# Attention's values as matmuls over two-part operands, and a paced output product

## The chip, the cores and the metric

The program runs on one NeuronCore of a Trainium2 chip. The metric is the time of one execution on the device in microseconds (us); lower is better. TensorE is called PE here, its weight loads PEld, VectorE DVE, ScalarE ACT, GpSimd POOL, and the DMA queue of SyncE SP.

## The reference, cut to what matters

The model is a two-layer trunk. In each layer one projection of the normalised input feeds three branches (a gated linear recurrence, sparse attention and a state-space scan), and one output product adds their concatenation to x:

```python
qg = qq.reshape(Bn, qb, N_KV_HEADS, G, ATT_HEAD_DIM)
logits = jnp.einsum('bqgrd,bqkgd->bqgrk', qg, ksel).astype(jnp.float32) * (ATT_HEAD_DIM ** -0.5)
...
p = jax.nn.softmax(logits, axis=-1)
o = jnp.einsum('bqgrk,bqkgd->bqgrd', p.astype(vsel.dtype), vsel)
...
y_b = o * jax.nn.silu(ga)
...
mix = jnp.concatenate([y_a, y_b, y_c], axis=-1)
x = x + jnp.einsum('bte,ed->btd', mix, p['w_out'].astype(mix.dtype)).astype(x.dtype)
```

There are 1024 prompt tokens and 64 sample tokens with 512 cached ones. Attention has 8 query heads in 2 key groups of 4, each 64 wide. The output product maps 2048 inputs to 1024 outputs for 1088 tokens.

## The kernel before

All values are float32. The large products run in PE's single-pass form (fp32r): an operand is split into a high part, rounded by a copy into an fp32r tile, and a low part, the rest, by a subtraction. `three` (lines 212 to 217) adds high by high, high by low and low by high into one PSUM bank. Attention's product of weights with values is not of this kind: it runs on float32 operands as they are.

Tokens come in chunks of 384, 384 and 320 columns (`CH`) for the projections, and in nine query tiles for attention: eight of 128 prompt tokens and one, tile 8, of 64 sample tokens.

A layer ends with attention and the output product. The output product is done in two halves (half 0 and half 1, or product 0 and product 1), each of 8 inputs of 128 rows: half 0 takes the recurrence's outputs and half of the scan's, which are ready before attention; half 1 takes the rest of the scan's and attention's. `y_tile` loads one input chunk and splits it into the tiles `Y` (names sth and stl in the profile: high and low; a holds chunks 0 and 1, b chunk 2). There is one set of these tiles, used by half 0 and then by half 1. `out_proj(half, ...)` goes over 8 blocks d of 128 outputs: `weights` loads and splits 128x1024 weights (whi by ACT, wlo by POOL), and for each chunk 24 matmuls go into a bank mm, which `add_x` (half 0) or `add_last` (half 1) adds to x.

Attention works on units of one query tile and one key group, 18 of them, in the order of `todo`: group 0 with tiles 1, 0, 2, 3, 4, 5, 8, 7, 6, then group 1 with 2, 1, 0, 3, 8, 4, 5, 6, 7. Tile t below 8 reaches 128 (t+1) keys, tile 8 reaches 576. `queries` transposes a unit's queries. `weigh` computes, for each of 4 heads, scores in PSUM (L1068), adds bias and mask and takes the minimum on DVE (L1071), exponentiates on ACT (L1075, with the sum), and scales by the reciprocal on DVE (L1077, L1078). `values` takes the weights 128 keys at a time: four transposes into a bank tp (L1093), a copy to pT on ACT (L1095), and the products with the values vt (L1098) into a bank s1; at the end DVE multiplies by the gate (L1100) and two DMAs store to ybd. Each L1098 product has 64 output rows and lies in one half of the array's columns: b = 0 and b = 1 write partitions 0 to 63 and 64 to 127.

The order of instructions on each engine is fixed before the run by a planner that simulates the program. The program's text gives priority: half 0 stands after all of attention, so its matmuls fill places where, in the planner's simulation, none of attention's is ready. Weights are given a higher priority (`high_priority`). The pool `p` has two buffers of each tile unless said otherwise; eight of lg, the 128x1024 tiles of weights. PSUM has three banks mm, two tp, two s2 (scores) and one s1.

## Time and profile before

| what | value |
|---|---|
| median of three runs | 2049.99 us (2048.08 to 2056.05) |
| the profiled execution | 2043.88 us, span 2042.1 us, mean granted clock 0.983 |
| busy share of the span | PE 96%, PEld 86%, DVE 74%, ACT 60%, POOL 32% |
| attention with half 0, layer 0 | about 690 to 948 us of the span |
| the same, layer 1 | about 1700 to 1955 us |

Times inside the span are counted from its first instruction. The busy time of PE is modelled: matmuls are pipelined and overlap, so that a busy PE can still have empty places; its weight loads show these better. A group's idle time is that of its engine just before it, with what ended it. An fp32 operand shows as f32, an fp32r one also as f32 on PE. An instruction of PE on an fp32 product appears twice.

### The profile page before, as it was taken

The page shows a single profiled execution, that of the slowest core. Times are in us where ns is not written, and L with a number is a line of the kernel's source. Part 1 is how long each engine was busy: PE and PEld are TensorE (multiplying, and loading weights), DVE is VectorE, ACT ScalarE, POOL GpSimd, SP SyncE. Part 2 cuts the span into 40 slices and gives each one's busy share as a digit, 9 for nine tenths or more (in the row PEclk, how much of TensorE's full clock was granted, in tenths as well). Part 3 has the DMA queues.
Part 4 walks back from the last instruction along what each step waited for, and adds up shares of the span by engine and source line. Part 5 has one row for each costly group of instructions (what it writes and reads, how often), then busy time and mean ns, then how long its engine had stood idle before and what let it go on. Part 6 is the DMA issues. An engine that isn't in the chain of part 4 may idle for free.

```text
span 2042.1 us, 34620 instructions
## 1 busy us (share of the span) xinstructions
PE 1952.6 (96%) x12056; PEld 1747.9 (86%) x12056; DVE 1519.2 (74%) x3701; ACT 1231.8 (60%) x2567; POOL 651.2 (32%) x561
## 2 busy tenths in 40 slices
PE   6999999989999899999999999999899999999999
PEld 5899989888889787866998999999888887888589
DVE  7778899898866855574386888999987678566723
ACT  6569988753656544454355798987446655444621
POOL 3012244333522422253430213353245224223320
PEclk9999999999999899999999999999999998999999
DMA  6125354535332732324541343545353346234145
GB/s 228 62 72 143 101 167 123 173 105 154 107 109 83 231 116 89 106 89 137 191 134 38 108 124 108 161 137 165 99 163 97 96 149 197 90 99 140 46 145 169
DMA packets 252079, 257.94 MB, mean 126 GB/s; under 512 B 31264, under 2 KB 230304, under 8 KB 251904
## 3 DMA queue, kind: packets, MB, share of 16 engines
q1 hardware_dynamic: 251904, 255.73, 40.9%
q8 instruction: 95, 1.56, 0.3%
q14 instruction: 80, 0.66, 0.1%
HBM read 181.09 MB, written 74.57 MB: 125 GB/s over the span
## 4 chain that ended last, share of the span: by engine, by line
PE 66%; DVE 19%; DMA 6%; ACT 5%; issue 3%; SPq 1%; POOL 0%; DVEq 0%; ACTq 0%
PE mm L216 16%; PE mm L215 15%; PE mm L217 15%; PE s L1098 4%; PE tp L1093 4%; PE s L1068 3%; DVE u L855 2%; ACT junka L580 2%; PE s L881 1%; DMA cumB<-cumd 1%; PE s L514 1%; DMA eB<-cumd 1%; ACT cumB L742 1%; DMA xsc<-xsd 1%; PE s L791 1%
## 5 line engine op out<-in xcount | busy, mean ns | idle before, releaser
L193 POOL TENSOR_TENSOR wlo<-wraw,whi 128x1024 fp32r<-128x1024 f32 x80 | 195.4, 2442 | 364.0 <-ACT whi L192 360.3
L580 ACT ACTIVATE junka<-sc,cand 128x768 bf16<-128x768 f32 x248 | 239.4, 968 | 8.5 <-DVE sc L583 3.9
L192 ACT ACTIVATE whi<-wraw 128x1024 fp32r<-128x1024 f32 x130 | 137.1, 1054 | 135.3 <-PE mm L216 109.8
L1075 ACT ACTIVATE lg<-lg,mx 128x512 f32<-128x512 f32 (+8 forms) x144 | 111.2, 773 | 95.7 <-DVE mx L1071 95.3
L855 DVE SCALAR_TENSOR_TENSOR u<-raw,parh,u 128x384 f32<-128x384 f32 (+1 forms) x198 | 147.4, 751 | 11.7 <-POOL u L853 5.9
L1095 ACT ACTIVATE pT<-tp 128x512 f32<-128x512 f32 (+1 forms) x164 | 90.5, 568 | 108.1 <-PE tp L1093 103.5
L1060 POOL TENSOR_TENSOR nbm<-nb,shared 128x256 f32<-128x256 f32 (+1 forms) x112 | 81.2, 730 | 224.1 <-DVE mx L1071 201.8
L574 DVE TENSOR_SCALAR_CACHE_REDUCE junk<-sc,cand 128x384 bf16<-128x384 f32 (+4 forms) x194 | 139.9, 753 | 1.0
L1068 PE MATMUL s<-kst,qst 128*128 128x512 f32 (+4 forms) x448 | 120.8, 362 | 7.8 <-DVE mx L1071 7.3
L742 ACT ACTIVATE cumB<-cumB,ctk 128x128 f32<-128x128 f32 (+1 forms) x288 | 88.4, 384 | 54.3 <-DMA cumB<-cumd 47.7
L1093 PEld LDWEIGHTS tp<-identr,lg 128*128 128x128 f32 (+2 forms) x656 | 71.8, 140 | 45.6 <-issue 39.4
L1093 PE MATMUL tp<-identr,lg 128*128 128x128 f32 (+2 forms) x656 | 107.2, 278 | 0.5 <-DVE lg L1078 0.5
L1098 PE MATMUL s<-pT,vt 128*64 128x256 f32 (+2 forms) x656 | 104.8, 389 | 1.6 <-ACT pT L1095 1.6
L1078 DVE TENSOR_SCALAR lg<-lg,ri 128x512 f32<-128x512 f32 (+8 forms) x144 | 93.6, 651 | 3.3
L1143 DVE TENSOR_TENSOR xl<-xl,mm 128x384 f32<-128x384 f32 (+1 forms) x40 | 21.4, 540 | 94.1 <-PE mm L217 84.9
L1068 PEld LDWEIGHTS s<-kst,qst 128*128 128x128 f32 (+1 forms) x448 | 72.2, 188 | 21.9 <-DVE mx L1071 13.4
L215 PE MATMUL mm<-sth0a,whi 128*128 128x384 f32 (+1 forms) x228 | 82.9, 365 | 7.3 <-DVE xl L1143 2.0
L1071 DVE CUSTOM_DVE_ANT_0 lg<-s,shared 128x512 f32<-128x512 f32 (+4 forms) x112 | 61.8, 553 | 37.7 <-PE s L1068 31.9
L193 DVE TENSOR_TENSOR wlo<-wraw,whi 128x1024 fp32r<-128x1024 f32 x50 | 64.1, 1281 | 32.1 <-ACT whi L192 32.0
L216 PE MATMUL mm<-stl1a,whi 128*128 128x384 f32 (+1 forms) x228 | 79.6, 349 | 3.8 <-DVE stl1a L954 3.5
L216 PE MATMUL mm<-stl0a,whi 128*128 128x384 f32 (+1 forms) x228 | 79.8, 350 | 2.4 <-POOL stl0a L954 2.0
L778 POOL TENSOR_TENSOR hT<-hT,dec 128x512 f32<-128x512 f32 x28 | 35.9, 1282 | 144.3 <-DVE hT L780 137.0
(475 smaller groups left out, 6931.1 us busy)
## 6 DMA issues: line engine op xcount, KB each, us to landing
wraw<-in_w_in_dram SPq DMA_DIRECT2D x82, 512.0 KB, 3.5
wraw<-in_w_out_dram SPq DMA_DIRECT2D x48, 512.0 KB, 3.8
cumB<-cumd SPq DMA_DIRECT2D x32, 512.0 KB, 4.8
xsd<-u SPq DMA_DIRECT2D x48, 192.0 KB, 2.4
gz<-gzd SPq DMA_DIRECT2D x32, 256.0 KB, 3.6
xsc<-xsd SPq DMA_DIRECT2D x32, 256.0 KB, 3.5
eB<-cumd SPq DMA_DIRECT2D x56, 128.0 KB, 4.1
gzd<-g SPq DMA_DIRECT2D x32, 192.0 KB, 1.9
```

Of the source, the lines that this page charges most:

```text
L192: S.activation(hi, raw, AF.Copy)
L193: eng.tensor_tensor(lo, raw, hi.bitcast(F32), op=OP.subtract)
L215: PE.matmul(ps, hi[:, k, :], xh[ci][:, c0:], start=k == 0, stop=False)
L216: PE.matmul(ps, hi[:, k, :], xl[ci][:, c0:], start=False, stop=False)
L217: PE.matmul(ps, lo[:, k, :], xh[ci][:, c0:], start=False, stop=k == len(xs) - 1)
L574: V.tensor_scalar(junk, sc[j][:n], thr, None, op0=op, op1=OP.add, accum_out=out)
L580: S.activation(junk, sc[j][:n], AF.Sign, scale=-1.0, bias=cand, accum_out=out)
L855: V.scalar_tensor_tensor(u, raw[:, j:j + n], w[:, wbase + j * wstride:wbase + j * wstride + 1], u, op0=OP.mult, op1=OP.add)
L1068: PE.matmul(ps[:nq, :b - a], qst[:, h, :nq], kst[:, g, pt, kbase + a:kbase + b], start=pt == 0, stop=pt == 1)
L1075: S.activation(lg[:nq, :nk], lg[:nq, :nk], AF.Exp, scale=-1.0, bias=mx[:nq, h, k_ - 1:k_], accum_out=sm[:nq, h:h + 1])
L1093: PE.transpose(ps[:n, i * nq:(i + 1) * nq], lgs[h][:nq, j * 128:j * 128 + n], ident[:nq, :nq])
L1098: PE.matmul(av[64 * b:64 * b + 64, :, :nq], vt[:n, vj, 64 * g:64 * g + 64], pT[:n, 2 * b:2 * b + 2, :nq], start=j == 0, stop=j == nb_ - 1)
```

## The change

Four things change.

1. The values are split once at the start of attention into vhl: for each group 64 columns of high parts and 64 of low parts. They are loaded into two lg buffers and split by ACT and POOL. The transposed weights are split too: pT holds the high part (ACT's copy, now fp32r, three buffers instead of two), pl the low part (a DVE subtraction that reads PSUM). One 128-key step has two matmuls instead of two fp32 ones: 128 columns of vhl by pT, then by pl, each for all four heads (512 columns). The bank s1 then has high-value sums in partitions 0 to 63 and low-value sums in 64 to 127, for four heads; two ACT copies move what is needed across partitions into sm2, two DVE additions add the other part, and DVE multiplies by the gate from SBUF.
2. `weigh` scales every other head (h odd) on ACT instead of DVE.
3. `out_proj` of half 0 gets `behind`: the matmuls of block d stand on PE after the last values matmul of the unit by which (d-1)/8 of attention's work (keys reached, summed over units) is done. Blocks 0 and 1 are free.
4. The `y_tile` calls of half 1's chunk 2 move from before its `out_proj` to after its block d = 2; their ACT and DVE instructions stand behind that block's weight copy and addition.

`tc.issue_after(ins)` keeps the instructions in its block behind `ins` on the engine of `ins`.

```diff
--- before.py
+++ after.py
@@ -180,6 +180,8 @@
         V.tensor_scalar(z, x, sign, 0.0, op0=OP.mult, op1=OP.max)
         V.scalar_tensor_tensor(out, q, 2.0, z, op0=OP.mult, op1=OP.add)
 
+    marks = {}
+
     def load(block):
         raw = wts.tile([128, 1024], F32, name="wraw", bufs=RB)
         SP.dma_start(raw, block)
@@ -189,7 +191,7 @@
 
         hi = wts.tile([128, 1024], F32R, name="whi")
         lo = wts.tile([128, 1024], F32R, name="wlo")
-        S.activation(hi, raw, AF.Copy)
+        marks["split"] = S.activation(hi, raw, AF.Copy)
         eng.tensor_tensor(lo, raw, hi.bitcast(F32), op=OP.subtract)
         return hi.rearrange("p (k c) -> p k c", k=8), lo.rearrange("p (k c) -> p k c", k=8)
 
@@ -953,18 +955,19 @@
                 S.activation(Y[k][0][ci], s_, AF.Copy)
             (V if k % 8 in YL else G).tensor_tensor(Y[k][1][ci], s_, Y[k][0][ci].bitcast(F32), op=OP.subtract)
 
-        def out_proj(half, Y, chunks, done, eng=G):
+        def out_proj(half, Y, chunks, done, eng=G, behind=None):
 
             for d in range(8):
                 ws = weights(I["w_out"][l, half, d], eng)
                 for ci in chunks:
                     a, b = CH[ci]
                     ps = mm_bank()
-                    three(ps[:, :b - a], ws, Y, ci)
+                    with behind(d) if behind else ExitStack():
+                        three(ps[:, :b - a], ws, Y, ci)
                     done(d, ci, a, b, ps)
 
         kst = kp.tile([128, 2, 2, TP + PAST + TS], F32R, name="kst")
-        vt = kp.tile([128, 13, 128], F32, name="vt")
+        vhl = kp.tile([128, 13, 2, 128], F32R, name="vhl")
         def near_bias(g):
 
             nb = kp.tile([128, 4, 256], F32, name="nb")
@@ -977,9 +980,15 @@
 
         nb = near_bias(0)
 
-        SP.dma_start(vt[:, 0:8, :], kvd[:, 0:8, 128:256])
-        SP.dma_start(vt[:, 8:12, :], I["cache_att_v"][l])
-        SP.dma_start(vt[:TS, 12, :], kvd[:TS, 8, 128:256])
+        v0, v1 = [p.tile([128, 1024], F32, name="lg", bufs=8) for _ in range(2)]
+        v0, v1 = [v.rearrange("p (t c) -> p t c", c=128) for v in (v0, v1)]
+        SP.dma_start(v0, kvd[:, 0:8, 128:256])
+        SP.dma_start(v1[:, 0:4, :], I["cache_att_v"][l])
+        SP.dma_start(v1[:TS, 4, :], kvd[:TS, 8, 128:256])
+        for v, n, a, b, c in ((v0, 128, 0, 8, 0), (v1, 128, 8, 12, 0), (v1, TS, 12, 13, 4)):
+            v = v[:n, c:c + b - a].rearrange("p t (g c) -> p t g c", g=2)
+            S.activation(vhl[:n, a:b, :, 0:64], v, AF.Copy)
+            G.tensor_tensor(vhl[:n, a:b, :, 64:128], v, vhl[:n, a:b, :, 0:64].bitcast(F32), op=OP.subtract)
         kf, kc_ = [p.tile([128, 1024], F32, name="lg", bufs=8) for _ in range(2)]
         kf = kf.rearrange("p (t c) -> p t c", c=128)
         SP.dma_start(kf, kvd[:, 0:8, 0:128])
@@ -990,7 +999,7 @@
 
             n = TS if t0 == 12 else 128
             kb_ = (ks_ if t0 == 12 else kf)[:n, t0 % 12:t0 % 12 + w, 64 * g:64 * g + 64][:, :, None, :].to_broadcast([n, w, 2, 64])
-            khl = p.tile([128, 2, 4, 64], F32R, name="pT")
+            khl = p.tile([128, 2, 4, 64], F32R, name="pT", bufs=3)
             S.activation(khl[:n, :w, 0:2, :], kb_, AF.Copy)
             V.tensor_tensor(khl[:n, :w, 2:4, :], kb_, khl[:n, :w, 0:2, :].bitcast(F32), op=OP.subtract)
             ps = tp_bank()
@@ -1075,7 +1084,10 @@
                 S.activation(lg[:nq, :nk], lg[:nq, :nk], AF.Exp, scale=-1.0, bias=mx[:nq, h, k_ - 1:k_],
                              accum_out=sm[:nq, h:h + 1])
                 V.reciprocal(ri[:nq, h:h + 1], sm[:nq, h:h + 1])
-                V.tensor_scalar(lg[:nq, :nk], lg[:nq, :nk], ri[:nq, h:h + 1], None, op0=OP.mult)
+                if h % 2:
+                    S.activation(lg[:nq, :nk], lg[:nq, :nk], AF.Copy, scale=ri[:nq, h:h + 1])
+                else:
+                    V.tensor_scalar(lg[:nq, :nk], lg[:nq, :nk], ri[:nq, h:h + 1], None, op0=OP.mult)
             return lgs
 
         def values(t, g, lgs):
@@ -1084,20 +1096,30 @@
             nk = reach(t)[1]
             ga = p.tile([128, 2, 128], F32, name="ga", bufs=1)
             SP.dma_start(ga[:, :, :nq], gad[:, 2 * g:2 * g + 2, t * 128:t * 128 + nq])
-            av = s1_bank()[:, :256].rearrange("p (r q) -> p r q", r=2)
+            av = s1_bank().rearrange("p (r q) -> p r q", r=4)
             nb_ = (nk + 127) // 128
             for j in range(nb_):
                 n = min(128, nk - 128 * j)
                 ps = tp_bank()
                 for i, h in enumerate((0, 2, 1, 3)):
                     PE.transpose(ps[:n, i * nq:(i + 1) * nq], lgs[h][:nq, j * 128:j * 128 + n], ident[:nq, :nq])
-                pT = p.tile([128, 4, 128], F32, name="pT")
-                S.activation(pT[:n, :, :nq], ps[:n, :4 * nq].rearrange("p (r q) -> p r q", r=4), AF.Copy)
+                ps = ps[:n, :4 * nq].rearrange("p (r q) -> p r q", r=4)
+                pT = p.tile([128, 4, 128], F32R, name="pT", bufs=3)
+                pl = p.tile([128, 4, 128], F32R, name="pl")
+                S.activation(pT[:n, :, :nq], ps, AF.Copy)
+                V.tensor_tensor(pl[:n, :, :nq], ps, pT[:n, :, :nq].bitcast(F32), op=OP.subtract)
                 vj = j + (8 if t == 8 else 0)
-                for b in range(2):
-                    PE.matmul(av[64 * b:64 * b + 64, :, :nq], vt[:n, vj, 64 * g:64 * g + 64], pT[:n, 2 * b:2 * b + 2, :nq],
-                              start=j == 0, stop=j == nb_ - 1)
-            V.scalar_tensor_tensor(ga[:, :, :nq], av[:, :, :nq], 0.5, ga[:, :, :nq], op0=OP.mult, op1=OP.mult)
+                for k_, w in enumerate((pT, pl)):
+                    marks["av"] = PE.matmul(av[:, :, :nq], vhl[:n, vj, g, :], w[:n, :, :nq], start=j == 0 and k_ == 0,
+                              stop=j == nb_ - 1 and k_ == 1)
+
+            sm2 = p.tile([128, 2, 128], F32, name="sm2", bufs=1)
+            S.activation(sm2[0:64, :, :nq], av[64:128, 0:2, :nq], AF.Copy)
+            S.activation(sm2[64:128, :, :nq], av[0:64, 2:4, :nq], AF.Copy)
+            for b in range(2):
+                c = slice(64 * b, 64 * b + 64)
+                V.tensor_tensor(sm2[c, :, :nq], sm2[c, :, :nq], av[c, 2 * b:2 * b + 2, :nq], op=OP.add)
+            V.scalar_tensor_tensor(ga[:, :, :nq], sm2[:, :, :nq], 0.5, ga[:, :, :nq], op0=OP.mult, op1=OP.mult)
             for i in range(2):
                 SP.dma_start(ybd[2 * g + i][:, t * 128:t * 128 + nq], ga[:, i, :nq])
 
@@ -1112,6 +1134,8 @@
         ws_ = [weigh(*todo[0], qs[0])]
         run(PLAN[4])
         all_keys(1)
+
+        work, done_ = 0, []
         for i, (t, g_) in enumerate(todo):
             if i + 2 < len(todo):
                 qs.append(queries(*todo[i + 2]))
@@ -1120,11 +1144,17 @@
             if i + 1 < len(todo):
                 ws_.append(weigh(*todo[i + 1], qs[i + 1]))
             values(t, g_, ws_[i])
+            work += reach(t)[1]
+            done_.append((work, marks["av"]))
         Y = [stream(k) for k in range(8)]
         for ci in range(3):
             for k in range(8):
                 y_tile(Y, yad + ycd[0:4], k, ci)
-        out_proj(0, Y, (0, 1, 2), add_x, EA)
+
+        def behind(d):
+            ins = [m for w, m in done_ if w <= work * (d - 1) / 8]
+            return tc.issue_after(ins[-1].ins) if ins else ExitStack()
+        out_proj(0, Y, (0, 1, 2), add_x, EA, behind)
         stA.close()
         obp = pool(stQ, L("OB"))
 
@@ -1140,7 +1170,7 @@
                 x_ = xpool.tile([128, 320], F32, name=f"Xc{d}")
                 X[d, ci] = x_
             SP.dma_start(x_, xd[d][:, a:b])
-            V.tensor_tensor(x_, x_, ps[:, :w], op=OP.add)
+            marks["xl"] = V.tensor_tensor(x_, x_, ps[:, :w], op=OP.add)
             if not last:
                 SP.dma_start(xd[d][:, a:b], x_)
                 if d == 0:
@@ -1155,10 +1185,18 @@
         stX = ExitStack()
         stX.enter_context(stQ)
         srcs = ycd[4:8] + ybd
-        for ci in range(3):
+        for ci in range(2):
             for k in range(8):
-                y_tile(Y, srcs, k, ci, ci == 2)
-        out_proj(1, Y, (0, 1), add_last, EB)
+                y_tile(Y, srcs, k, ci)
+
+        def add_early(d, ci, a, b, ps):
+            add_last(d, ci, a, b, ps)
+            if d == 2 and ci == 1:
+
+                with tc.issue_after(marks["split"].ins), tc.issue_after(marks["xl"].ins):
+                    for k in range(8):
+                        y_tile(Y, srcs, k, 2, True)
+        out_proj(1, Y, (0, 1), add_early, EB)
         if not last:
             xpool = pool(stX, L("X"))
             sqs.append(xpool.tile([128, 384], F32, name="sqs2"))
```

## Rows read from the trace of the kernel before

**Rows 1.** The page's part 1: engine, busy us (share of the span) x instructions
```profile
PE 1952.6 (96%) x12056; PEld 1747.9 (86%) x12056; DVE 1519.2 (74%) x3701; ACT 1231.8 (60%) x2567; POOL 651.2 (32%) x561
```

**Rows 2.** The page's part 4: shares of the chain that ended last
```profile
PE 66%; DVE 19%; DMA 6%; ACT 5%; issue 3%; SPq 1%; POOL 0%; DVEq 0%; ACTq 0%
```

**Rows 3.** Windows: length, busy PE, PEld, DVE, ACT, POOL (instructions); granted clock, DMA share, GB/s
```profile
200.00:300.00 100.00, 96.98 (x620) 93.50 (x618) 93.00 (x227) 88.51 (x192) 34.12 (x24) 1.00 0.41 125
660.00:700.00 40.00, 33.03 (x171) 28.92 (x170) 31.24 (x95) 18.96 (x50) 16.73 (x15) 0.79 0.75 243
700.00:880.00 180.00, 180.00 (x1145) 145.80 (x1144) 108.16 (x351) 87.60 (x186) 56.45 (x59) 1.00 0.39 120
880.00:900.00 20.00, 19.10 (x117) 14.22 (x115) 12.47 (x37) 8.19 (x20) 11.48 (x11) 1.00 0.23 70
900.00:948.00 48.00, 44.67 (x278) 25.27 (x276) 31.06 (x104) 31.62 (x59) 12.79 (x13) 1.00 0.16 49
```

**Rows 4.** The same view for instructions on mm alone: PE, PEld, DVE, ACT
```profile
700.00:880.00 180.00, 108.35 (x553) 90.30 (x552) 12.67 (x24) 0.00 (x0) 1.00 0.39 120
...
900.00:948.00 48.00, 1.54 (x6) 0.96 (x6) 0.00 (x0) 0.00 (x0) 1.00 0.16 49
```

**Rows 5.** Timeline of PE near attention's end: start us, us, what
```profile
939.92 1.08 PE L1098 MATMUL s<-pT,vt 128*64 128x256 f32 x8
940.93 0.66 PE L1093 MATMUL tp<-identr,lg 128*128 128x128 f32 x4
941.52 0.65 PE L1098 MATMUL s<-pT,vt 128*64 128x256 f32 x4
942.10 0.66 PE L1093 MATMUL tp<-identr,lg 128*128 128x128 f32 x4
```

**Rows 6.** Timeline of PE in the middle of attention
```profile
804.01 0.33 PE L217 MATMUL mm<-sth2a,wlo 128*128 128x384 f32 x1
804.19 0.34 PE L215 MATMUL mm<-sth3a,whi 128*128 128x384 f32 x1
804.45 0.65 PE L1098 MATMUL s<-pT,vt 128*64 128x256 f32 x4
805.04 0.66 PE L1093 MATMUL tp<-identr,lg 128*128 128x128 f32 x4
805.45 0.42 PE L216 MATMUL mm<-stl3a,whi 128*128 128x384 f32 x1
805.71 0.63 PE L1068 MATMUL s<-kst,qst 128*128 128x512 f32 x2
806.17 0.33 PE L217 MATMUL mm<-sth3a,wlo 128*128 128x384 f32 x1
```

**Rows 7.** Groups of PE by shape: xcount | busy us, mean ns | idle before
```profile
L1098 PE MATMUL s<-pT,vt 128*64 128x128 f32 x64 | 7.2, 296 | 0.0
```

**Rows 8.** The page's part 5, DVE's scaling of the weights
```profile
L1078 DVE TENSOR_SCALAR lg<-lg,ri 128x512 f32<-128x512 f32 (+8 forms) x144 | 93.6, 651 | 3.3
```

**Rows 9.** Groups of DVE by shape, 690 to 955
```profile
L1071 DVE CUSTOM_DVE_ANT_0 lg<-s,nbm,mx 128x256 f32<-128x256 f32 x48 | 22.7, 481 | 5.0 <-PE s L1068 2.6 <-DVE mx L1071 0.7
L1071 DVE CUSTOM_DVE_ANT_0 lg<-s,shared 128x512 f32<-128x512 f32 x24 | 16.5, 686 | 7.9 <-PE s L1068 7.8
L1071 DVE DVE_READ_ACCUMULATOR2_ANT mx<- 128x1 f32 x125 | 10.2, 82 | 0.0
L1077 DVE RECIPROCAL ri<-sm 128x1 f32<-128x1 f32 x62 | 9.7, 158 | 22.4 <-ACT lg L1075 22.2
...
L1100 DVE SCALAR_TENSOR_TENSOR ga<-s,ga 128x256 f32<-128x256 f32 x16 | 6.7, 418 | 14.3 <-PE s L1098 11.8 <-DMA ga<-gad 2.3
```

**Rows 10.** Groups of ACT by shape, 690 to 955
```profile
L192 ACT ACTIVATE whi<-wraw 128x1024 fp32r<-128x1024 f32 x9 | 9.5, 1052 | 3.8 <-issue 3.2 <-PE mm L216 0.6
...
L1028 ACT ACTIVATE qhl<-qn 128x256 fp32r<-128x256 f32 x13 | 5.3, 409 | 0.5 <-DMA qn<-qnd 0.5
```

**Rows 11.** Groups of POOL, 690 to 955
```profile
L954 POOL TENSOR_TENSOR stl3a<-g,sth3a 128x384 fp32r<-128x384 f32 x3 | 3.1, 1030 | 1.5 <-DMA g<-ybd 1.0 <-DVE sth3a L951 0.5
```

## The prediction

> **What bounds the kernel now.** I read the busy line of the page first: TensorE (PE) is busy 96% of the span, the next engine, DVE, 74% [rows 1]. The chain that ended last agrees: two thirds of it is PE [rows 2]. So a microsecond of PE work removed is a microsecond of the program, wherever PE has other work ready. The windows show where that holds in the stage that the change touches, attention with the output product's first half (layer 0; layer 1 repeats it). From 700 to 880 PE is busy all the time and DVE 108 of 180 us; from 900 to 948 PE is busy 44.7 of 48, but its weight loads only 25.3; and the start, 660 to 700, is thin on PE, at a granted clock of 0.79 [rows 3]. The next view says why the last part differs: the projections' accumulator mm sees 553 matmuls from 700 to 880 and 6 from 900 to 948 [rows 4]. Product 0 is used up as filler by about 880, and the last 50 us of attention run with nothing beside them.
>
> Then one looks at the instructions that the change replaces, the product of transposed weights with values (L1098). I call 128 keys of one query tile and one key group a block; it has four transposes (L1093) and four L1098 instructions (two fp32 products, two instructions each). There are 36 + 5 blocks in a group, 82 in a layer, 164 in all: 144 with 128 queries, 20 with 64.
>
> **The change part by part, for both layers.** *A, the product.* From out_proj's matmul at 804.19 to the transposes at 805.04 is 0.85 us; one step of such a matmul is 0.18 (804.01 to 804.19), so the product takes 0.67 [rows 6]. Beside transposes it is dearer: the period of four transposes and a product is 1.17 (940.93 to 942.10 [rows 5]), and four transposes alone take 0.41 (805.04 to 805.45 [rows 6]), which leaves 0.76. The new product is two single-pass matmuls of 512 columns; the score matmuls L1068 have this form, and two take 0.46 (805.71 to 806.17 [rows 6]). So 0.21 to 0.30 is saved 144 times, 30 to 43 us. The 20 small blocks: 16 of them cost 7.2 us, 0.45 each [rows 7], against two matmuls of half the columns, 0.23: 4 us. I take A = -36, nearer the first, since two thirds of the stage has out_proj beside it; bounds -47 and -30, the latter because some blocks stand in pairs, two at 1.01 (939.92 to 940.93 [rows 5]).
>
> Those rows show a price of switching: a lone product costs 0.67 or more, a second one directly behind it some 0.4. The Trainium skill, TensorEngine Tiling (Array Packing), has a rule for each side. Its Theoretical Speedup section gives up to 2x to a left operand of at most 64 columns, which speaks against this change, since it gives such tiles up; its Key Properties say that changing the tiling mode drains the engine, which speaks for it. By the first alone the new product would save nothing; by both it saves A. The trace has both.
>
> *B, the work put on DVE and ACT.* In a layer DVE gains 72 subtractions pl of 128x512 out of PSUM; the nearest row, L1071 of that size with its sum in PSUM, takes 0.69 [rows 9]: 50 us, and 10 small ones, 4. It gains two additions a unit (18 units; each 64x256, as L1100's 0.42 [rows 9]): 15. It loses every other L1078, 36 of 0.651 [rows 8]: -23. Net +46. From 700 to 948 DVE is busy 151.8 of 248 [rows 3]; with A's 18 us gone, 198 of 230, or 86%. ACT gains those 36 scalings (mean width 576; between 0.409 at 256 and 1.052 at 1024 columns [rows 10], so 0.68): 24, and 36 copies of 64x256 at 0.41: 15; it goes from 127 to 166 of 230. PE's own work covers both, since from 200 to 300 this kernel ran DVE at 93 of 100 with PE at 97 [rows 3]. Cost 0 on the average of the stage; what is not covered is in C and E.
>
> *C, the order.* `behind` holds block d of product 0 until (d-1)/8 of the attention work is done. In the middle an eighth then has 230/8 = 29 us of PE against DVE's 198/8 = 25: PE stays the bound. The end: d=7 comes free after tile 4 of group 1, at 7680 of 10368 columns; tiles 5, 6, 7 remain, 21 blocks. DVE has there 21 x 0.69 = 14.5 for pl; 2.5 for three combinations; the scores of tile 7, tile 6 and half of tile 5, at 2.6, 2.3 and 1.8 us a head (pieces of 0.686 and 0.481, 0.35 for a third of 128 columns estimated from these, reads of 0.082, a reciprocal of 0.158 [rows 9], half an L1078): 23; about 7 for splitting product 1's inputs and adding x: 47 us. PE has 21 x (0.41 + 0.46) = 18; scores 8; d=7 itself 48 x 0.18 + 24 x 0.15 (320 of 384 columns) = 12: 38. So some 9 us of PE idle, where 880 to 948 now has 68 - 63.8 = 4 [rows 3]: +5 if nothing else fills, below 0 if product 1's first block gets in. I take +2 a layer, +4 (-8, all idle time covered, to +20).
>
> *D, the values' split at the start.* ACT gets copies of 1024, 512 and 128 columns, about 2 us [rows 10], and POOL subtractions of the same, about 4 (L954 takes 1.03 for 384 [rows 11]), in the thin stretch 660 to 700; the DMAs move the same bytes. Behind POOL's 4 us wait the low halves for out_proj's first matmuls. Mostly covered by DMA waits there; +1 a layer, +2 (0 to +8).
>
> *E, one accumulator bank.* The next unit's first product now waits for two copies (0.82) and two additions (0.84) instead of one L1100 (0.42): 1.3 us later. Scores, transposes and out_proj cover it except at the last three units: 1.3 x 6 = 8; I take half, +4 (0 to 47, all 36 units bare). The tp bank is held for copy and subtraction, 0.7 longer; two banks at one block in 2.8 us (230 over 82) leave room: 0. The third pT buffer alone: 0, the work above covers it either way. The last y_tile group behind d=2 moves 8 loads on SP and 16 conversions that are needed only by the last 192 x 0.15 = 28 us of the layer: 0; the inputs' loads and stores of x no longer queue behind them on SP.
>
> Sum: -36 + 0 + 4 + 2 + 4 = -26. The profiled execution took 2043.9 (span 2042.1); the median of the runs shown is 2050.0, 6 more. The changed kernel comes to 2018 in that execution's terms and **2024** as a median.
>
> **The rivals.** *Product 1's inputs come late (slower).* Y has one set of buffers: product 1's splits overwrite what d=7 reads. Now product 0 ends by 880 [rows 4], so they run under attention. If d=7's matmuls are left until attention ends, its 12 us stand uncovered, and then ten POOL subtractions of 1.03 [rows 11] and their loads, about 13 us, leave PE empty: 25 a layer, 50 in all, 2050 - 36 + 50 = 2064. It decides once d=7 ends less than 13 us before attention. For it: PE's order is fixed by the planner's own idea of DVE's speed. Against it: PE idles 9 us or more there, which is what a filler takes. 0.09.
>
> *DVE becomes the bound.* Each block's second matmul now waits for transposes, ACT, then DVE, which runs in order, with instructions of up to 1 us ahead. If that makes DVE's 25 us an eighth 29, it equals PE; 0.25 us of queueing a block (164 x 0.25 = 41) eats A: about 2050, within 10 us. For it: the end, 47 against 38. Against it: the 93 in rows 3. 0.17.
>
> *The filler covers the end as well.* The 4 idle us a layer go and A is at its upper bound: 2050 - 47 - 8 = 1995. For it: a filler is exactly what 900 to 948 lacks. Against it: DVE's 47 us. 0.12.
>
> *Tiles of 64 columns were the better form.* If blocks mostly ran behind each other at 0.4, the product would save nothing and the other terms stay: +10, 2060. Rows 5 and 6 show lone blocks; a pair is the exception. 0.02. This would be the Trainium skill's first rule above (TensorEngine Tiling, Theoretical Speedup); the trace bears it out for pairs alone.
>
> **How the numbers follow.** The forecast, 10 to 45 us faster, has 0.60; its own range is 2005 to 2040. With 0.12 for the covered end, 0.17 around no change (0.04 of it past -10) and 0.11 slower, faster by over 0.5% (10 us, about what a measurement of this kernel can tell) is 0.76, same 0.13, slower 0.11. The range 1996 to 2046 takes in A's upper bound with the end covered, and A's lower bound with C at +20 and 6 from D and E; some 0.2 lies outside, most of it above.
>
> **What the profile would show.** A: the values' products in pairs about 0.23 apart, no idle weight loads around them, and PE's busy time down. B: DVE near 200 of 230 in the stage, ACT near 166. C: mm matmuls spread to the stage's end instead of 6 in its last 50 us; PE waiting for pl or L1071 at tiles 6 and 7. Late inputs: a hole of over 10 us between d=7 and product 1. The prediction is wrong if the stage (700 to 948) is not 8 to 20 us shorter in each layer, or if other stages move by more than a few us.

## The result and the profile after

The changed kernel takes 2066.8 us (median of 4 runs, 2064.9 to 2073.9) where the kernel before takes 2049.0 in the same comparison: a ratio of 1.0095, 95% interval 1.0077 to 1.0112. It is slower by 0.9%; the forecast was 2024. The profiled execution of the changed kernel has a span of 2062.7, 20.6 more than before.

The first view is the page's busy line, as in [rows 1]:

```profile
PE 1934.1 (94%) x11728; PEld 1775.6 (86%) x11728; DVE 1594.8 (77%) x3865; ACT 1305.9 (63%) x2717; POOL 659.1 (32%) x567
```

PE has 18.5 us less to do and the program is 20.6 longer, so PE stands idle for 39 us more by the record. The same windows as in [rows 3], and one behind them, say where (length, busy PE, PEld, DVE, ACT, POOL, granted clock, DMA share, GB/s):

```profile
660.00:700.00 40.00, 24.73 (x121) 21.48 (x121) 23.30 (x61) 14.37 (x31) 17.88 (x15) 0.70 0.68 212
700.00:880.00 180.00, 171.95 (x1029) 149.21 (x1029) 143.46 (x458) 122.76 (x275) 52.18 (x58) 0.99 0.34 103
...
900.00:948.00 48.00, 44.25 (x250) 38.24 (x249) 35.88 (x90) 29.79 (x52) 19.64 (x17) 1.00 0.37 114
948.00:968.00 20.00, 16.96 (x85) 15.53 (x86) 5.67 (x11) 5.41 (x10) 5.38 (x4) 0.91 0.68 221
```

The start has lost 8.3 us of PE, and the middle, where PE was busy all of 180 us, another 8. The view for mm alone, as in [rows 4], shows that the pacing did what it says; the filler now reaches the end:

```profile
700.00:880.00 180.00, 90.70 (x459) 76.11 (x459) 10.57 (x20) 0.00 (x0) 0.99 0.34 103
880.00:900.00 20.00, 7.57 (x42) 6.69 (x42) 0.49 (x1) 0.00 (x0) 1.00 0.28 82
900.00:948.00 48.00, 24.73 (x124) 20.87 (x122) 1.56 (x3) 0.00 (x0) 1.00 0.37 114
```

Times of some instructions on the two timelines cut the 20.6 us into pieces (start of the instruction, us):

```
                               layer 0            layer 1
                            before   after     before   after
PE   first key transpose     667.6   684.5     1674.3  1700.5
PE   first values matmul     704.1   715.6     1712.5  1731.6
PE   last values matmul      947.3   951.1     1954.9  1970.8
DVE  last add of x (xl)     1037.1  1044.8     2038.8  2059.4
```

Up to the first values matmul 11.5 us are lost in layer 0 and 11.4 more in layer 1 (1712.5 - 1037.1 = 675.4 against 686.8). Between the first and the last values matmul 7.7 and 3.2 us are won. From there to the last add 3.9 and 4.7 are lost. Sum: 22.9 - 10.9 + 8.6 = 20.6.

**The start.** SP's queue, before (first fence) and after (second): start us, duration, line.

```profile
660.25 0.39 SPq L985 DMA_DIRECT2D lg<-kvd  x1
660.74 0.65 SPq L986 DMA_DIRECT2D lg<-in_cache_att_k_dram  x1
...
674.25 0.37 SPq L980 DMA_DIRECT2D vt<-kvd  x1
```

```profile
672.79 0.38 SPq L985 DMA_DIRECT2D lg<-kvd  x1
673.23 0.85 SPq L986 DMA_DIRECT2D lg<-in_cache_att_v_dram  x1
...
674.65 1.17 SPq L994 DMA_DIRECT2D lg<-kvd  x1
675.86 2.94 SPq L995 DMA_DIRECT2D lg<-in_cache_att_k_dram  x1
```

The keys' two loads went out at 660.3 and 660.7, 14 us ahead of the values'. Now the values' first load goes out at 672.8 and the keys' stand behind it, at 674.7 and 675.9. PE's timeline shows who waits:

```profile
676.26 0.52 PE L219 MATMUL mm<-sth1a,wlo 128*128 128x384 f32 x1
684.54 0.68 PE L1008 MATMUL tp<-identr,pT 128*128 128x128 f32 x2 [7.76 <-ACT pT L1003]
```

**Inside attention.** One window from the first to the last values matmul, layers 0 and 1; before, then after:

```profile
704.10:947.60 243.50, 239.61 (x1506) 181.41 (x1505) 147.34 (x476) 124.70 (x258) 77.81 (x79) 1.00 0.33 101
1712.50:1955.30 242.80, 237.29 (x1509) 183.74 (x1508) 152.04 (x478) 124.93 (x259) 75.77 (x79) 1.00 0.33 102
```

```profile
715.60:951.50 235.90, 224.07 (x1313) 192.02 (x1311) 182.01 (x551) 156.51 (x321) 69.93 (x73) 0.99 0.32 98
1731.60:1971.20 239.60, 225.73 (x1313) 193.47 (x1312) 182.69 (x549) 157.25 (x321) 69.51 (x73) 0.99 0.32 96
```

PE has 193 instructions fewer in layer 0's window; 164 are the product, which has half as many, so 29 of the output product's matmuls stand elsewhere (the view for mm alone counts 594 and 565), 5 us at their step of 0.17 (948.93 to 949.10 under The end); in layer 1 it is 32, 5.5 us. PE's busy time falls by 15.5 and 11.6, hence by 10.5 and 6 from the product itself. PE's idle time (length less busy) rises from 3.9 to 11.8 and from 5.5 to 13.9, by 16.3 in all: what the product saves, 16.5, goes into idle time, and the 10.9 us by which the stretch is shorter are the filler that moved out of it.

PE's timeline in the middle shows how a block runs now:

```profile
762.06 0.39 PE L1113 MATMUL s<-pT,vhl 128*128 128x512 f32 x1
762.29 0.31 PE L219 MATMUL mm<-sth5b,wlo 128*128 128x320 f32 x1
...
763.03 0.39 PE L1113 MATMUL s<-pl,vhl 128*128 128x512 f32 x1
763.26 0.39 PE L1113 MATMUL s<-pT,vhl 128*128 128x512 f32 x1
763.49 0.49 PE L1105 MATMUL tp<-identr,lg 128*128 128x128 f32 x3
763.74 0.48 PE L1113 MATMUL s<-pl,vhl 128*128 128x512 f32 x1
```

Where nothing is waited for, a matmul takes the 0.23 of the forecast (763.03 to 763.26, 763.26 to 763.49). The two of a block stand apart, with other work between them while DVE makes pl. The waits that the view names, layer 1 (us in total, times, longest):

```profile
PE s L1077 <- DVE mx L1080: 5.4, 4, 2.0
PE s L1113 <- DVE pl L1110: 2.5, 12, 0.4
PE s L1113 <- DVE sm L1121: 2.5, 3, 1.3
```

These three, the longest, are for DVE; three more, 2.5 us together, are for ACT. The instructions themselves cost what was forecast (DVE by shape, xcount, busy us, mean ns; 0.69 and 0.42 were taken from [rows 9]):

```profile
L1110 DVE TENSOR_TENSOR pl<-tp,pT 128x512 fp32r<-128x512 f32 x144 | 98.2, 686 | 24.3 <-ACT pT L1109 23.6
...
L1121 DVE TENSOR_TENSOR sm<-sm,s 64x256 f32<-64x256 f32 x64 | 26.6, 416 | 8.5 <-ACT sm L1118 7.9
```

**The end.** PE's timeline behind the last values matmul, before and after:

```profile
948.65 0.44 PE L215 MATMUL mm<-sth0a,whi 128*128 128x384 f32 x1 [0.99 <-DVE xl L1143]
948.93 0.34 PE L216 MATMUL mm<-stl0a,whi 128*128 128x384 f32 x1
949.10 0.34 PE L217 MATMUL mm<-sth0a,wlo 128*128 128x384 f32 x1
```

```profile
951.09 0.50 PE L1113 MATMUL s<-pl,vhl 128*128 128x512 f32 x1
954.38 0.69 PE L217 MATMUL mm<-sth0a,whi 128*128 128x384 f32 x1 [2.79 <-DVE xl L1173]
954.87 0.52 PE L218 MATMUL mm<-stl0a,whi 128*128 128x384 f32 x1
955.18 0.52 PE L219 MATMUL mm<-sth0a,wlo 128*128 128x384 f32 x1
```

The banks mm wait for the additions xl, and these stand on DVE behind the last unit's combination. After 2.8 idle us the matmuls are 0.31 apart where they were 0.17: the granted clock from 954.3 to 957 is 0.50, the lower of the two levels, 1.2 GHz (before, 948.6 to 951: 1.00), and in 948 to 968 the mean is 0.91.

### The profile page after: what moved, and what is told of

Its sections match the earlier page's. It is cut to its first block, busy times and chain, and to the rows that moved or that the text cites. A ratio compares the mean times of both kernels' runs of the same rounds, so it can differ in the third digit from the quotient of the medians.

```text
span 2062.7 us, 34206 instructions
## 1 busy us (share of the span) xinstructions
PE 1934.1 (94%) x11728; PEld 1775.6 (86%) x11728; DVE 1594.8 (77%) x3865; ACT 1305.9 (63%) x2717; POOL 659.1 (32%) x567
## 5 line engine op out<-in xcount | busy, mean ns | idle before, releaser
L1109 ACT ACTIVATE pT<-tp 128x512 fp32r<-128x512 f32 (+1 forms) x164 | 89.8, 564 | 57.6 <-PE tp L1105 55.5
L1110 DVE TENSOR_TENSOR pl<-tp,pT 128x512 fp32r<-128x512 f32 (+1 forms) x164 | 106.2, 653 | 25.1 <-ACT pT L1109 24.2
L1105 PE MATMUL tp<-identr,lg 128*128 128x128 f32 (+2 forms) x656 | 101.7, 270 | 2.6 <-ACT lg L1088 2.3
L217 PE MATMUL mm<-sth0a,whi 128*128 128x384 f32 (+1 forms) x228 | 84.5, 371 | 18.5 <-DVE sth0a L953 7.5
L1105 PEld LDWEIGHTS tp<-identr,lg 128*128 128x128 f32 (+2 forms) x656 | 78.8, 140 | 22.1 <-ACT lg L1088 3.2
L218 PE MATMUL mm<-stl3a,whi 128*128 128x384 f32 (+1 forms) x228 | 79.0, 346 | 2.3 <-POOL stl3a L956 2.3
L217 PE MATMUL mm<-sth3a,whi 128*128 128x384 f32 (+1 forms) x228 | 79.2, 347 | 0.5 <-DVE sth3a L953 0.5
L217 PE MATMUL mm<-sth2a,whi 128*128 128x384 f32 (+1 forms) x228 | 79.1, 348 | 0.5 <-DVE sth2a L953 0.5
```

The costliest lines, as they stand in the source:

```text
L217: PE.matmul(ps, hi[:, k, :], xh[ci][:, c0:], start=k == 0, stop=False)
L218: PE.matmul(ps, hi[:, k, :], xl[ci][:, c0:], start=False, stop=False)
L1105: PE.transpose(ps[:n, i * nq:(i + 1) * nq], lgs[h][:nq, j * 128:j * 128 + n], ident[:nq, :nq])
L1109: S.activation(pT[:n, :, :nq], ps, AF.Copy)
L1110: V.tensor_tensor(pl[:n, :, :nq], ps, pT[:n, :, :nq].bitcast(F32), op=OP.subtract)
```

## The experiments

Each run stands against runs of the kernel before on the same chip. The chip differs between groups of runs, so it is the ratios that compare, not the medians; 1% is 20.5 us. "After" is the changed kernel. The theories, in the order in which they came up: S, the late start; P, the pacing leaves PE without filler; W, PE stands waiting for pl; H, the subtraction holds the transposes' bank; L, DVE's load as such.

```
run                     median   ratio to before, 95% interval
after                   2066.8   1.0095  1.0077 to 1.0112
e1_keys_first           2080.3   1.0135  1.0106 to 1.0163
e2_sm2_k                2069.6   1.0093  1.0061 to 1.0125
e3_both                 2064.8   1.0058  1.0032 to 1.0083
e4_no_behind            2076.6   1.0121  1.0095 to 1.0147
f1_pl_unread            2072.2   1.0088  1.0063 to 1.0113
f2_no_pl                2049.3   0.9985  0.9970 to 1.0001
f4_values_alone         2088.2   1.0170  1.0149 to 1.0191
g1_before_pad           2059.6   1.0029  1.0011 to 1.0047
h1_pl_from_sbuf         2077.6   1.0132  1.0111 to 1.0154
h2_pool_scaling         2066.3   1.0073  1.0050 to 1.0096
h3_pool_scaling_start   2055.9   1.0031  1.0011 to 1.0051
k1_without_products     2037.4   0.9935  0.9912 to 0.9958
m1_dve_load             2045.3   0.9958  0.9938 to 0.9979
m3_no_behind            2053.6   0.9997  0.9976 to 1.0018
m4_no_early             2032.8   0.9903  0.9876 to 0.9930
m5_dve_scaling          2045.3   0.9967  0.9950 to 0.9984
n1_no_pl_start          2045.5   0.9979  0.9960 to 0.9998
n2_pool_no_early        2036.8   0.9933  0.9915 to 0.9950
```

**The start: order or place.** In the program, attention's pool p is 7168 bytes a partition larger than before. It begins at byte 103136 (110304 before), and the scan's pool ends at 103648, so the first lg buffer shares 512 bytes with the scan's last tile. e1 changes the order, e2 the place, e3 both.

```diff
 e1: the block from "v0, v1 = ..." to the end of its split
     moved behind all_keys(0)
 e2:
-            sm2 = p.tile([128, 2, 128], F32, name="sm2", bufs=1)
+            sm2 = kp.tile([128, 2, 128], F32, name="sm2", bufs=1)
```

> The changed kernel with the values' loads and split moved behind the keys' (the keys are then loaded first, as in the kernel before). Theory S (the start: keys' loads are queued behind the values' and land 14 to 20 us later than before, about 11.5 us a layer): if the order of the loads alone is at fault, 2067 - 2 x 11.5 = 2044, first key transpose of layer 0 at about 668 (684.5 in the changed kernel). If instead the place in memory is at fault (the first of these tiles shares bytes with the scan's last tile, and now that is the keys' tile), less than 5 us are gained: 2062 to 2067, with the keys' transposes still after 680. Rival theory P (pacing: the output product held back by the rule that ties its blocks to attention leaves PE without filler, 13 to 32 us idle a layer): no change but what the start gives.

> The changed kernel with one tile (sm2, 1024 bytes a partition) allocated in the other pool of attention, so that the pool of the loads' tiles is 1024 bytes shorter and no longer shares bytes with the scan's last tile; the order of the loads stays (values, then keys). Theory S, memory: the values' first load is issued some 10 us earlier and the keys' behind it; 2067 - 15 to 23 = 2044 to 2052. Theory S, order: no gain, 2065 to 2068. Theory P: no gain.

> Both edits: keys' loads first, and sm2 in the other pool. Theory S in either form: the start goes back to that of the kernel before, first key transpose near 668, first values' product near 704 in layer 0: 2067 - 23 = 2044 (2040 to 2049). If it gives less than 10 us, the start was not what costs the time, and theory P or another holds: the late start was only shifted idle time that the rest would have had anyway.

SP's queue in e1 (L985 and L986 are the keys' loads there), then in e2 (L994 and L995):

```profile
675.28 0.38 SPq L985 DMA_DIRECT2D lg<-kvd  x1
675.72 0.99 SPq L986 DMA_DIRECT2D lg<-in_cache_att_k_dram  x1
```

```profile
660.87 0.39 SPq L985 DMA_DIRECT2D lg<-kvd  x1
...
662.59 0.58 SPq L994 DMA_DIRECT2D lg<-kvd  x1
663.26 1.02 SPq L995 DMA_DIRECT2D lg<-in_cache_att_k_dram  x1
```

It is the place: in e2 the pool begins at 104160, above the scan's end. With the keys first, their load still goes out only at 675.3; with the pool 1024 bytes shorter, the values' first load goes out at 660.9 and the keys' 1.7 later. (e1 is 0.4% slower than after; why stays open.) The first key transpose is back at 670.7. Yet e2 is no faster than after, and e3 by 0.37%, with intervals that touch. Attention starts 10 us earlier and takes longer (its windows, layers 0 and 1):

```profile
705.40:949.50 244.10, 231.61 (x1337) 199.11 (x1335) 186.54 (x560) 157.64 (x322) 70.93 (x75) 0.97 0.32 96
1721.10:1969.70 248.60, 232.48 (x1354) 199.64 (x1352) 187.11 (x564) 158.50 (x325) 73.96 (x78) 0.99 0.33 98
```

PE is idle for 12.5 and 16.1 us there, and product 1's first matmul comes 6.1 us behind the end of the last values matmul (2.8 in after), waiting for xl: in e2 the loads of x stand on SP behind the last unit's stores (952.6 behind 951.7; in after they went out at 945.5). So the late start is a fault of its own, but not what keeps the program long; theory S alone falls.

The kernel before with the late start alone:

```diff
+        pad = p.tile([128, 1792], F32, name="pad", bufs=1)
+        G.memset(pad[:, 0:1], 0.0)
         ks_ = kp.tile([128, 1, 128], F32, name="ks")
```

> The kernel before with an unused tile of 7168 bytes a partition in attention's pool, so that the pool reaches as far down as in the changed kernel and the first of its tiles, here the keys', shares bytes with the scan's last tile. Nothing else is changed. Theory S: the keys' first load is issued some 12 us later, first key transpose of layer 0 at about 680 in place of 667.6, and the program is 2 x 8 to 12 longer: 2065 to 2073. Rival (the late start is absorbed, since only filler moves): 2049 to 2055.

It costs 0.29% (0.11 to 0.47), 2 to 10 us in two layers: less than expected, and more than nothing.

**The pacing.**

```diff
-        out_proj(0, Y, (0, 1, 2), add_x, EA, behind)
+        out_proj(0, Y, (0, 1, 2), add_x, EA)
```

> The changed kernel without the rule that holds block d of product 0 until (d-1)/8 of attention is done (the order is then as in the kernel before). Theory P: PE's idle time inside attention (32 and 36 us by layer, 13 and 12 in the kernel before) goes back to about 13, product 1's first block comes in again under attention: 2067 - 15 to 25 = 2042 to 2052. Theory S alone: no change, 2063 to 2070. If the pacing helps as the prediction thought (its step C), it gets slower: 2072 to 2080.

Not faster, 0.26% slower than after, with intervals that overlap. In layer 0's window PE is idle for 14.6 us, against 11.8 in after. Theory P falls: PE's idle time in attention is not the pacing's doing.

**The wait for pl, or DVE's load.** f1 takes the wait away, f2 the work too, h1 leaves the work but frees the transposes' bank.

```diff
-                V.tensor_tensor(pl[:n, :, :nq], ps, pT[...], op=OP.subtract)      (f2: left out)
+                V.tensor_tensor(pl[:n, :, :nq], pT[...], pT[...], op=OP.subtract) (h1)
-                for k_, w in enumerate((pT, pl)):
+                for k_, w in enumerate((pT, pT)):                                 (f1, f2, h1)
```

> The changed kernel, with the product's second matmul reading pT a second time in place of pl; DVE still computes pl, which nobody reads (so the values' product leaves out its low part). PE's work and DVE's work are those of the changed kernel; only the wait for pl is gone. Theory W (each block's second matmul waits for the transposes, ACT's copy and then DVE's subtraction, and PE, which runs in order, stands): values' matmuls and the steps behind them give back most of the 14 to 17 us a layer by which they exceed 0.23 us each; 2067 - 20 to 30 = 2037 to 2047. Rival L (DVE is simply overloaded, whatever waits for pl): at most 5 us: 2062 to 2067. Rival S (late start alone): no change.

> As the one before, and DVE's subtraction is left out as well (106 us of DVE's time in the program are gone; the low part of the values' product is left out). Theory W: the same as with pl unread, within 8 us (2032 to 2047). Rival L: only here does the time come back, 2067 - 30 to 40 = 2027 to 2037, at least 15 less than with pl unread. Both small (above 2060): the stage is not bound by pl in any way, and theory S or the end remains.

> As the run with pl unread, and DVE's instruction now reads pT in SBUF twice in place of the transposes in PSUM (the low part of the values' product is left out; pl is not read). DVE still does one instruction of 128x512 a block, but it holds no PSUM bank and nothing waits for it. Theory L (DVE is in order and simply has too much to do, so that score banks and copies behind it come free late): no better than with pl unread, 2062 to 2075. Rival H (the subtraction holds the transposes' bank longer, and PE's next transposes wait for that): back to the time without pl, 2045 to 2055.

Without the wait nothing is won: f1 is at 1.0088, and PE is idle for 12.4 and 17.0 us in its windows, against 11.8 and 13.9 in after. Without the work 1.1%, 22 us, come back. h1 is as slow as after or slower; its instruction takes 0.764 where pl's takes 0.686, so it has some 11 us more of DVE:

```profile
L1110 DVE TENSOR_TENSOR pl<-pT 128x512 fp32r<-128x512 f32 x144 | 108.7, 764 | 14.3 <-ACT pT L1109 14.0
```

Theory W falls. H falls too: even without these 11 us h1 would lie far above the 2045 to 2055 that H gave it. L stands in this kernel: the subtraction costs 21 to 22 us, whoever waits for it. f2's windows:

```profile
718.30:944.00 225.70, 217.46 (x1313) 192.31 (x1311) 136.79 (x466) 156.02 (x319) 70.27 (x73) 0.98 0.34 101
1726.30:1955.90 229.60, 220.52 (x1312) 193.15 (x1311) 138.94 (x473) 156.34 (x321) 69.46 (x73) 0.98 0.33 98
```

The same 1313 instructions occupy PE for 217.5 and 220.5 us where they occupied it for 224.1 and 225.7. I read this as matmuls that follow each other at once, against matmuls that the record stretches over short waits; busy time of PE is modelled, and no run shows it directly. Attention's window is 10 us shorter in each layer.

**The product alone, and the change without it.** f4 is e2 without pacing, without scaling on ACT and with the last inputs at their old place. k1 is after with the values' lines of the kernel before (vt, L1098); pacing, scaling on ACT, late inputs and third buffer stay.

> The values' product of two parts alone: without the rule that paces the output product, without the moved last inputs, without the scaling on ACT, and with sm2 in the other pool so that the start is that of the kernel before. What the prediction's term A with B, D and E would give by itself. By the prediction 2049 - 36 + 2 + 4 = 2019. Theory W: the waits for pl eat all of it, and DVE has 23 us a layer more to do: 2060 to 2085. If it is 2049 or below, the fault lies in the other parts of the change.

> The changed kernel with the values' product of the kernel before (tiles of 64 columns, no split): what is left of the change is the pacing of the output product, the scaling of odd heads on ACT, the late inputs behind d=2 and the third buffer. Theory L (the product of two parts costs more on DVE than it gives on PE): these parts by themselves take 5 to 20 us off the kernel before, 2030 to 2045. If they gain only by mending what the product does to DVE: 2045 to 2052. If the pacing hurts where PE has no idle time to lose: above 2055.

This tells most. The product alone makes the program 1.7% slower; all else without it makes it 0.65% faster. Put beside each other, the product costs 1.6%, 33 us (1.0095 against 0.9935). Attention in k1:

```profile
705.60:943.70 238.10, 235.29 (x1514) 184.25 (x1513) 130.72 (x443) 146.22 (x290) 71.62 (x76) 1.00 0.33 101
1714.00:1947.70 233.70, 233.04 (x1503) 182.51 (x1502) 129.10 (x445) 146.32 (x291) 70.00 (x75) 1.00 0.34 103
```

PE is idle for 2.8 and 0.7 us.

**Which of the other parts gains.** k1 without one part each: m3 without `behind`, m4 with the last inputs at their old place, m5 with every scaling on DVE.

> The change without the products and without the pacing of the output product: what the pacing gives. In the changed kernel taking it out cost 10 us. If it gives the most of the 13 us here too: 2045 to 2050; if the scaling on ACT does: 2034 to 2041.

> The change without the products and with the last inputs split at their old place. The prediction's step put this at nothing: 2034 to 2041. If the conversions stood in the way of product 1's start: 2042 to 2047.

> The change without the products and with all scalings on DVE. By theory L 23 us a layer more on DVE, against 54 a layer that cost 17 in all when pl was in: 2037 + 4 to 10 = 2041 to 2047. If DVE has room enough without pl: 2034 to 2040.

The pacing gives 0.62%, 13 us, clear of the intervals. The scaling on ACT gives about 0.3% and the moved inputs cost about 0.3%; each of these two intervals overlaps k1's. m4 beats both kernels: 2032.8, ratio 0.9903.

**DVE's load by itself.**

```diff
 k1 with, behind the copy of pT:
+                pl = p.tile([128, 4, 128], F32, name="pl")
+                V.tensor_tensor(pl[:n, :, :nq], ps[...], pT[:n, :, :nq], op=OP.subtract)
```

> The change without the products (2037), with one DVE subtraction of 128x512 a block added, written to a tile that nobody reads; PE's work and all else is that of the kernel without the products. Theory L (DVE's load alone, 164 x 0.65 = 106 us, slows attention): 2037 + 12 to 25 = 2049 to 2062, with DVE near 205 of 240 us in attention and PE's steps for scores and transposes longer. Rival (the load matters only together with the shorter PE work or the longer dependence chain of the new product): 2034 to 2043.

The load costs 0.23% there, some 5 us, with overlapping intervals, where it costs 22 with the new product. Load alone is not enough: it matters beside the new product. Whether that is by PE's shorter work or by the longer combination, no run separates.

**Relief for DVE.** The even heads' scaling goes to POOL, in after (h2), in e2 (h3) and in m4 (n2).

```diff
                 else:
-                    V.tensor_scalar(lg[:nq, :nk], ...)
+                    G.tensor_scalar(lg[:nq, :nk], ...)
```

> The changed kernel with the scaling of the even heads on POOL (DVE in the changed kernel, 23 us a layer): the full computation. DVE falls from 211 to about 188 of 235 us a layer in attention, POOL rises from 70 to about 125. Theory L: half of what leaving pl out gave (54 us of DVE a layer gave 17 us in all): 2067 - 7 to 15 = 2052 to 2060. Rival H, or POOL's longer latency and its queue in front of the split weights: 2065 to 2085.

> The scaling on POOL and sm2 in the other pool, so that the start of attention is that of the kernel before too: the full computation. Theory L with S (the padded kernel before lost 6 to 10 us by the late start): 2040 to 2055, the first that could equal the kernel before. If the start is absorbed again as with the kernel that only moved sm2, the time is that of the scaling on POOL alone.

> The full computation, without the products, with the last inputs at their old place, and the scaling of the even heads on POOL. The scaling of the odd heads on ACT gave some 7 us; if DVE's load still costs: 2033 - 3 to 7 = 2026 to 2030. If DVE is no bound any more: 2031 to 2036. If POOL's queue holds up the split weights: above 2038.

h2 is 0.2% faster than after, less than the interval. h3 is the best kernel with the whole new product, and still 0.3% slower than before. Against e2, which has its place of sm2, h3 gains 0.62%, 13 us, clear of the intervals: once attention starts early, relief for DVE does pay. In n2, where DVE has room, the relief gives nothing (0.9933 against 0.9903).

**The product without its price on DVE.** n1 is e2 without pl (as in f2) and with the last inputs at their old place; m4 is the same without the product.

> The changed kernel without DVE's subtraction (pT is read twice in its place, so the low part of the values' product is left out), with sm2 in the other pool (the start as before) and the last inputs at their old place. To be read against the same kernel without the products, 2033. If term A of the prediction is right and only DVE's load and the start stood against it: 2033 - 25 to 36, plus up to 8 for the longer combination: 1997 to 2016. If PE does not gain that much even then (its time goes into other waits): 2020 to 2040.

Slower than m4 by 0.76%, 16 us, and above both ranges of the expectation; the two profiled executions are 8.9 us apart. Attention's windows, m4 and then n1, and PE's longest wait in layers 0 and 1, m4 and then n1:

```profile
701.40:941.50 240.10, 235.69 (x1514) 184.31 (x1513) 135.97 (x450) 147.64 (x293) 76.38 (x81) 1.00 0.34 104
1709.30:1944.30 235.00, 233.45 (x1503) 182.60 (x1502) 132.10 (x450) 147.11 (x292) 74.49 (x79) 1.00 0.34 105
```

```profile
705.10:936.90 231.80, 220.77 (x1337) 194.61 (x1335) 146.12 (x484) 158.35 (x324) 75.25 (x79) 0.99 0.35 104
1709.30:1946.40 237.10, 223.75 (x1351) 198.53 (x1349) 151.48 (x487) 159.87 (x328) 78.33 (x82) 0.99 0.35 106
```

```profile
PE s L1071 <- DVE mx L1074: 2.6, 4, 1.2
PE s L1071 <- DVE mx L1074: 1.0, 2, 0.7
```

```profile
PE s L1077 <- DVE mx L1080: 7.0, 10, 1.7
PE s L1077 <- DVE mx L1080: 9.2, 10, 2.7
```

n1's windows hold 13 matmuls of filler fewer in layer 0 and 12 more in layer 1. With this evened out at 0.18 each, PE's busy time falls by 12.6 and 11.8 us: term A is there, 24 us. PE's idle time rises from 4.4 to 11.0 and from 1.6 to 13.4: 18 of the 24 are gone. Some 13 of these 18 are waits of the scores for DVE to empty their banks, though DVE is busy only 63 to 64% of these windows.

The rest of the difference stands at the ends. The first values matmul comes 4 us later in each layer. Behind the last values matmul PE waits 6.1 us for xl in each layer, where m4 waits 1.0, since in n1, as in e2, the loads of x stand behind the stores; in layer 1 the last add comes 7 us later behind the last values matmul. That order is the planner's and no part of the product. So n1 is no clean price: some 5 to 10 of its 16 us can be this order.

## Why the prediction was wrong

**What failed: "B ... PE's own work covers both ... Cost 0 on the average of the stage."** Its durations were right (0.686 and 0.416 measured), its busy shares too high (182 and 157 of 236 measured, 198 and 166 of 230 forecast), and its conclusion wrong. The shares came out high because durations were added to a busy time in which DVE's records overlap: those of after's window sum to 212 us and occupy 182. Leaving out the 164 subtractions gives 22 us, and the whole product costs 33 (after against k1). The reason drawn from [rows 3], that this kernel can run PE at 97 and DVE at 93 of 100, was taken from a stage in which other work runs. In attention the engines hand each block on, scores to DVE to ACT to PE to ACT to DVE to PE, and PE stands when DVE is busy for 77% of the time. The rival "DVE becomes the bound", 2050 at 0.17, was nearest to this mechanism. It placed the price in the wait for pl, though, and f1 shows that without that wait PE waits elsewhere.

**A: right in kind, too large.** PE's busy time fell by 18.5 us in the program, 24 with pl out of the way (n1), against 36 forecast with bounds of 30 and 47. The prediction read the price of a lone product at two places. Over layer 0's window a lone one takes 0.58 from its start to the next instruction's (median of 57), two matmuls of the new form 0.47 (n1); and some 36 of the 164 blocks stood in pairs, where there is little to save. All of A came back as idle time in after, and three quarters in n1. The first sentence of the prediction's reading, that a microsecond of PE work removed is one of the program wherever PE has other work ready, has a condition that the change itself took away: with a shorter product PE has, at the places where it waits, no other work ready. The Trainium skill, Perfetto Trace Analysis, Identifying the Most-Contended Engine, warns that the busy time of matmuls is a poor measure of how close PE is to its limit. The traces agree: the same 1313 instructions read 224.1 us in after and 217.5 in f2, so part of the 96% in [rows 1] can be waits as well.

**D: +2 forecast, 23 seen at the first values matmul.** The step priced the split on ACT and POOL and said of the DMAs that they move the same bytes. It did not ask where their buffers lie, nor what is queued on SP behind them. The 7168 bytes by which the pool grew are the third pT buffer (2048), pl's two (4096) and sm2 (1024); the prediction put the third buffer at 0. By itself the late start costs 2 to 10 us (g1); in after, mending it gives 0 to 8 (e2, e3). Its own sign of being wrong came: attention's stretch was to be 8 to 20 us shorter in each layer, and it is 7.7 and 3.2, behind starts that are 11.5 and 11.4 later.

**C: +4 forecast, and the sign was wrong.** The pacing gains 13 us without the new product (m3 against k1); in the changed kernel it gains 5, within the intervals (e4). The filler does reach the end. No hole of over 10 us behind d=7 appeared, only the 2.8 above: "Product 1's inputs come late" is out, and its 2064 lies near the result by chance.

**E: about right inside attention, too small at the end.** PE's waits for the combination (L1121) are 2.2 and 2.5 us a layer, 4.7 in all where E had 4. What E left out is that the additions xl stand behind the last combination: from the last values matmul on, 3.9 and 4.7 us a layer are lost.

**The moved inputs, 0 forecast,** cost about 6 us, which the intervals don't settle.

**Left over.** By [rows 5], two blocks' products of 64 columns take 1.01 us together, and two of the new form 0.92 (4 times 0.23): behind each other the old product is nearly as good. The Trainium skill, TensorEngine Tiling (Array Packing), Theoretical Speedup, gives such tiles up to 2x, by which the new product would save nothing; in pairs the trace agrees within a tenth, 1.01 against 0.92. The rival built on it, 2060 at 0.02, is near the result by its number and not by its mechanism: pairs were a fifth of the blocks, and n1's 24 us show that lone blocks do gain.

What stays open in part is why the scores wait in n1 when DVE has 85 us free in each window. The timelines show what stands ahead of them in DVE's order. In layer 0 the gate's multiplication waits 2.77 us for its load (DMA ga<-gad), and PE's longest wait, 1.7, follows. In layer 1 waits of 2.7, 1.0 and 0.9 follow single instructions that take 2.3 to 2.6 us (L976, L956, L1121) where others of their form take 0.34 to 0.56, each beside a POOL subtraction of 128x1024. But m4 has as much of such lengthening in all, some 28 us in its two windows, and hardly waits. That n1 lacks other work for PE at these places is argued and not shown, and no run tells the combination's part from the planner's order.

## What to carry to other kernels

Work taken off the busiest engine is time only if the others can hand it the next block sooner, so price the whole round of a block, and let one run leave out the new work on the second engine before believing that it is covered. A pool that grows moves every tile in it: look at which older tile its first buffer now overlaps, and which loads are queued behind it. Run a change of several parts without its main part: here the pacing, put in beside the product, was worth 13 us by itself, and without the product and the moved inputs the kernel takes 2033 where the kernel before takes 2054 on the same chip.

## What the runs showed of the hardware

DVE's subtraction of 128x512 takes 0.69 us in the median, whether one operand is in PSUM (after) or both are in SBUF (h1, where they are the same tile). The means of 0.686 and 0.764 differ by what happens beside POOL. In after some 57 of the 164 subtractions overlap an instruction of POOL, and none takes more than 0.694 us. In h1 some 60 do, and some 25 of these take 0.77 to 2.72 us; every one longer than 0.72 stands beside a POOL instruction.

And 512 shared bytes a partition go with a load that is 12 us later (672.8 in after, 660.9 in e2): no row of a view names the place, only the two queues side by side show it.
